# A Conformer/S5 encoder trunk: the second MLP's second product and the final norm with tokens on partitions, three quarters of the product by Strassen's algorithm

## The chip, the cores and the metric

The kernel runs on one core of a Trainium2 chip. The metric is device time in microseconds (us) of one execution. Engines are named as in the profile: PE (TensorE, matmuls), PEld (its weight loads), DVE (VectorE), ACT (ScalarE), POOL (GpSimd), SP (the queue that starts most DMA transfers).

## The reference

One sequence of 512 tokens, 1024 channels, two layers. What matters here is the end of the second layer and the final norm; everything ahead of it (convolution and retention in layer 0, its MLP, the S5 state space layer and its gated unit) is untouched.

```python
h = _rmsnorm(x, norm_g[layer, 1]) * (1.0 + scale_f) + shift_f
x = x + gate_f * (jnp.square(jax.nn.relu(h @ w_fc1[layer])) @ w_fc2[layer])   # 1024 -> 4096 -> 1024
...
return _rmsnorm(x, norm_f)
```

All of it is float32. `gate_f` is one number for each channel.

## The kernel before

The residual stream `self.x` lies as eight tiles of 128 channels (partitions) by 512 tokens. A float32 product is made of three matmuls on halves: each operand is split into a rounded `hi` and a rest `lo` (type float32r), and `mm3` (line 198) adds hi x hi, hi x lo and lo x hi. A weight piece of 128 x 1024 is loaded by the SP queue (`load_unit`), its `hi` is a copy by ACT (line 194), its `lo` a subtraction by DVE (line 189); this is a split unit. `Stream` loads and splits some units ahead of use.

The MLP (`mlp`, line 756) goes through the 4096 hidden channels in four quarters. A quarter has eight units of the first product (24 matmuls each, weights stationary, the 512 tokens moving): relu and square on ACT (lines 801, 806), then split (lines 809, 810). Then eight units of the second product, one for each output tile of 128 channels; results of the first three quarters are partly held in PSUM (`held`), partly added to `self.x` by DVE at once (line 826, with the gate). At its beginning the reciprocal root of the norm (`rstd`) is hidden behind 48 matmuls on un-normed tiles of the first two units (`ahead`), and `norm_tiles` (lines 317 to 338) makes the eight normed tiles while four units run side by side (`group=[4, 1]`, line 817).

After the second MLP `run` (from line 1674) makes the final norm: squares are summed over channels by matmuls with a column of ones (`stats`, `col_sums`), DVE and ACT make the reciprocal root (`rsqrt`, lines 246 to 261), matmuls spread it over the partitions (`bcast`), DVE scales eight tiles (line 1679), and two queues write them out.

The order of instructions on each engine is a compiler's: it follows the program's order as priority, and pulls forward what is ready in its own timing model. Instructions marked `keep_in_program_order` (all SP loads among them) stay in order. Tiles come from pools with a fixed number of buffers (`ps`: eight PSUM banks; `wk`: eight work tiles; `wh` and `wl`: four each; `raw`: seven; `x`: ten).

## Time and profile before

| | |
|---|---|
| time, median of 3 runs | 1204.96 us (1204.0 to 1205.41) |
| profiled execution, its own time | 1205.55 us |
| its span, first to last instruction | 1203.8 us |
| mean granted clock of TensorE | 0.979 |
| busy, share of the span | PE 96%, DVE 72%, ACT 39%, POOL 9% |
| matmuls | 6830 |
| DMA | 223.58 MB, 186 GB/s mean |

The second MLP begins at about 840 us; its last matmul ends at 1188.7 us. A matmul's own duration overlaps with that of the next, so a busy PE says only that PE had no pause; its pace is read from the distance of starts. The granted clock is a share of 2.4 GHz. In a list of groups, `out<-in` are the program's tile names, then partitions x elements, the count, and after the bar busy time and mean duration of one in ns.

### The profile page before, as it was taken

Reading aid. Unit: us, or ns where it says so; the run is one execution under the profiler, and the core shown is the slowest. Engines: PE = TensorE matmul, PEld = TensorE weight load, DVE = VectorE, ACT = ScalarE, POOL = GpSimd, SP = SyncE. Lnnn points to the kernel's source line nnn. Section 1 sums busy time; section 2 is a strip of 40 time slices with the busy share of each in tenths; the row PEclk is TensorE's granted clock in tenths of the full one; section 3 lists DMA queues with packets and bytes.
Section 4 is the critical chain, followed back from the end, with each engine's and each line's share of the span. In section 5 each row is a group of like instructions: output and inputs, shape, how many; then the busy total and the mean of one; then the engine's idle time right before and its main releaser. Section 6 shows DMA issues by size and latency. Waiting matters only on the chain.

```text
span 1203.8 us, 17697 instructions
## 1 busy us (share of the span) xinstructions
PE 1160.8 (96%) x6830; PEld 929.4 (77%) x6830; DVE 864.0 (72%) x1602; ACT 470.5 (39%) x744; POOL 108.9 (9%) x222
## 2 busy tenths in 40 slices
PE   6999999999999999999999899999999999999996
PEld 4777756777888888878777678788888888888885
DVE  6899995999998898798968999498552332332343
ACT  4423322455523423512423756344451532422530
POOL 0000000000002222243422100000000000000000
PEclk7999999999999999999999989999999999999997
DMA  9755341545337689889797968376343333333201
GB/s 352 266 175 192 134 161 47 189 138 200 107 127 245 196 277 276 286 263 312 218 337 240 405 237 346 123 251 213 148 140 105 88 105 89 104 91 103 70 1 70
DMA packets 65668, 223.58 MB, mean 186 GB/s; under 512 B 11136, under 2 KB 11520, under 8 KB 63536
## 3 DMA queue, kind: packets, MB, share of 16 engines
q1 hardware_dynamic: 48528, 174.63, 42.2%
q0 software_dynamic: 16480, 46.79, 12.6%
q8 instruction: 53, 0.87, 0.3%
q10 hardware_dynamic: 576, 1.05, 0.2%
q14 instruction: 31, 0.25, 0.1%
HBM read 197.77 MB, written 29.82 MB: 189 GB/s over the span
## 4 chain that ended last, share of the span: by engine, by line
PE 82%; DVE 8%; DMA 6%; issue 2%; ACT 1%; SPq 0%; POOL 0%; DVEq 0%; POOLq 0%; ACTq 0%
PE ps L167 81%; DVE wk L1291 2%; DMA raw<-adn 1%; DMA d_wi<-eb 1%; DVE w L861 1%; DMA bt<-bt 1%; DVE wl L189 1%; DVE xt L1421 1%; DVE hx L1291 1%; DMA d_t<-d_kk 1%; PE ps L1247 1%; DVE eb L861 1%; DMA raw<-adt 1%; DMA raw<-fc 0%; DMA x<-x 0%
## 5 line engine op out<-in xcount | busy, mean ns | idle before, releaser
L194 ACT CAST wh<-raw 128x1024 fp32r<-128x1024 f32 x169 | 176.8, 1051 | 504.4 <-PE ps L167 439.5
L189 DVE TENSOR_TENSOR wl<-raw,wh 128x1024 fp32r<-128x1024 f32 x169 | 206.0, 1222 | 174.3 <-ACT wh L194 172.1
L167 PE MATMUL ps<-hh,wh 128*128 128x512 f32 x808 | 317.3, 399 | 3.7 <-ACT hh L334 1.7
L167 PE MATMUL ps<-hl,wh 128*128 128x512 f32 x808 | 317.5, 393 | 1.6 <-DVE hl L235 1.2
L167 PE MATMUL ps<-hh,wl 128*128 128x512 f32 x808 | 316.2, 392 | 0.8 <-DVE wl L189 0.8
L167 PE MATMUL ps<-fl,wh 128*128 128x512 f32 x544 | 212.4, 391 | 2.5 <-DVE fl L810 2.5
L167 PE MATMUL ps<-fh,wh 128*128 128x512 f32 x544 | 212.9, 393 | 0.0
L167 PE MATMUL ps<-fh,wl 128*128 128x512 f32 x544 | 212.3, 391 | 0.0
L167 PEld LDWEIGHTS ps<-hh,wh 128*128 128x128 f32 x808 | 152.4, 189 | 41.7 <-issue 3.1
L167 PEld LDWEIGHTS ps<-hl,wh 128*128 128x128 f32 x808 | 152.9, 189 | 34.3 <-DVE hl L235 1.6
L167 PEld LDWEIGHTS ps<-hh,wl 128*128 128x128 f32 x808 | 152.6, 189 | 33.6 <-DVE wl L189 1.6
L167 PEld LDWEIGHTS ps<-fl,wh 128*128 128x128 f32 x544 | 102.5, 188 | 24.4 <-DVE fl L810 3.5
L167 PEld LDWEIGHTS ps<-fh,wh 128*128 128x128 f32 x544 | 102.4, 188 | 22.0 <-issue 1.0
L167 PEld LDWEIGHTS ps<-fh,wl 128*128 128x128 f32 x544 | 102.4, 188 | 21.3
L535 DVE SCALAR_TENSOR_TENSOR cacc<-apad,cvw,cacc 128x512 f32<-128x512 f32 x120 | 83.7, 746 | 0.0
L826 DVE SCALAR_TENSOR_TENSOR x<-ps,mod,x 128x512 f32<-128x512 f32 x40 | 29.9, 748 | 63.1 <-PE ps L167 63.0
L810 DVE TENSOR_TENSOR fl<-wk,fh 128x512 fp32r<-128x512 f32 x64 | 44.1, 689 | 17.3 <-ACT fh L809 17.3
L277 ACT ACTIVATE wk<-x 128x512 f32<-128x512 f32 x35 | 22.1, 630 | 59.0 <-DVE x L826 30.2
L861 DVE TENSOR_TENSOR w<-pb,bt 128x512 f32<-128x512 f32 x64 | 41.4, 687 | 4.7 <-DMA bt<-bt 4.2
L433 DVE SCALAR_TENSOR_TENSOR raw<-raw,x 128x512 f32<-128x512 f32 x52 | 33.2, 687 | 11.9 <-DMA raw<-adt 9.3
L806 ACT ACTIVATE wk<-wk 128x512 f32<-128x512 f32 x64 | 40.7, 636 | 1.5
L809 ACT CAST fh<-wk 128x512 fp32r<-128x512 f32 x64 | 39.8, 622 | 1.7
(240 smaller groups left out, 1265.9 us busy)
## 6 DMA issues: line engine op xcount, KB each, us to landing
raw<-fc SPq DMA_DIRECT2D x128, 512.0 KB, 4.3
raw<-adn SPq DMA_DIRECT2D x50, 512.0 KB, 4.9
raw<-adt SPq DMA_DIRECT2D x34, 512.0 KB, 4.8
pb<-d_pw POOLq DMA_DIRECT2D x32, 256.0 KB, 8.6
bt<-bt POOLq DMA_DIRECT2D x16, 512.0 KB, 9.4
d_e<-eb POOLq DMA_DIRECT2D x16, 512.0 KB, 4.3
d_wi<-eb POOLq DMA_DIRECT2D x16, 512.0 KB, 8.1
wi<-d_wi SPq DMA_DIRECT2D x8, 1024.0 KB, 5.5
```

The lines of the kernel that those rows point to most:

```text
L167: i = self.nc.tensor.matmul(out, lhsT=lhsT, rhs=rhs, start=start, stop=stop, **kw)
L189: self.keep(self.nc.vector.tensor_tensor(lo, raw, hi.bitcast(F32), SUB))
L194: self.keep(self.nc.scalar.copy(hi, raw))
L277: nc.scalar.activation(sq, t, AF.Square)
L433: self.keep(nc.vector.scalar_tensor_tensor(half, half, 1.0, self.cb[k], MUL, MUL, accum_out=v[:, 2 * k + h:2 * k + h + 1]))
L535: nc.vector.scalar_tensor_tensor(ac, ap[:, t:t + S], cvw[:, i * TAPS + t:i * TAPS + t + 1], ac, MUL, ADD)
L806: nc.scalar.activation(f, r, AF.Square)
L809: nc.scalar.copy(hi, f)
L810: nc.vector.tensor_tensor(lo, f, hi.bitcast(F32), SUB)
L826: nc.vector.scalar_tensor_tensor(self.x[m], ps, gate[:, m:m + 1], self.x[m], MUL, ADD)
L861: V.tensor_tensor(o, x, y, op)
L1291: pin(nc.vector.tensor_tensor(*args))
```

## The change

`mlp(1)` and the final norm in `run` are replaced by `mlp_last`; the beginning of the MLP moves unchanged into `mlp_begin`, which both use. In `mlp_last`:

- The residual stream is transposed to tokens on partitions, four tiles `xt` of 128 tokens x 1024 channels, by 32 PE transposes and eight ACT copies.
- The second product has the hidden tile as the stationary operand and rows of `w_fc2` (128 x 1024, loaded as they are) as the moving one.
- Hidden channels 0 to 3071 go in four chunks of three pairs of 128. A pair's product, [512 tokens x 256] times [256 x 1024], is taken as 2 x 2 blocks of [256 x 128] and [128 x 512] by Winograd's form of Strassen's algorithm: `lefts` makes the sums and differences of hidden blocks and splits them, `right` those of weight blocks in place, `split_items` splits two of these at a time, and each of the seven products has two token tiles of three matmuls. Products 1, 6, 7 and 4 run on in the same two PSUM banks, 5 and 3 in two others, 2 in two more; after the last pair of a product `put` reads its banks and adds them to `cs`, eight tiles for the four output blocks. Each chunk has six first-product units ahead of its products, one of them (from the second chunk on) made ahead of product 4 of the chunk before, at `n == 18`.
- The last 1024 hidden channels are a plain product (`plain`) with eight PSUM banks, its weight rows multiplied by the gate ahead of the split. Meanwhile `add_sums` adds gate x `cs` to `xt`.
- The last three of its eight units are done for one token tile after the other, and each token tile is then normed (sums along the free dimension, by ACT) and written out.
- The gate reaches the free dimension through DRAM (`d_g`) on POOL's queue. The weight order is a list of loads and a list of splits (`Jobs`). The memory set aside for POOL's DMA descriptors is cut to 4096 bytes a partition.

```diff
+class Jobs:
...
+    def ahead(self, loads, splits):
+        while self.splits and len(self.ready) < splits:
+            f, n = self.splits.pop(0)
+            self.load(n)
+            self.ready.append(f())
+        if self.splits:
+            self.load(self.splits[0][1] + loads)
+    def __next__(self):
+        self.ahead(1, 1)
+        return self.ready.pop(0)
...
+    def mlp_last(self, out):
...
+        CH, NP, PL = 4, 3, 24
...
+        def row(u):
+            def f():
+                rows[u] = wr.tile([P, 1024], F32, name="wr", tag="wr")
+                self.load(rows[u], a["fc2_1"][u])
+            return f
...
+        def split_plain(u):
+            def f():
+                r = rows.pop(u)
+                for h in range(2):
+                    g = slice(h * 512, h * 512 + 512)
+                    V.tensor_tensor(r[:, g], r[:, g], gt[h], MUL)
+                return self.split_unit(r)
+            return f
...
+        def right(p, i):
+            r11, r12, r21, r22 = (reg(i, s, h) for s in range(2) for h in range(2))
+            if p == 1:
+                return r11
+            if p == 2:
+                return r21
+            if p == 3:
+                return r22
+            o, x, y = {5: (r11, r12, r11), 6: (r11, r22, r11), 7: (r12, r22, r12), 4: (r21, r21, r11)}[p]
+            V.tensor_tensor(o, x, y, SUB)
+            return o
+        slot = {1: 0, 2: 1, 4: 2, 5: 3, 6: 4, 7: 5, 3: 6}
+        items = [(1, 0), (1, 1), (5, 0), (5, 1), (1, 2), (5, 2)] + [(p, i) for p in (2, 6, 3, 7, 4) for i in range(NP)]
+        def split_items(q, its):
+            def f():
+                hi = self.wh.tile([P, 1024], F32R, name="wh", tag="wh")
+                lo = self.wl.tile([P, 1024], F32R, name="wl", tag="wl")
+                for n, (p, i) in enumerate(its):
+                    r, h = right(p, NP * q + i), slice(n * 512, n * 512 + 512)
+                    A.copy(hi[:, h], r)
+                    V.tensor_tensor(lo[:, h], r, hi[:, h].bitcast(F32), SUB)
+                return hi, lo
+            return f
...
+        loads, splits = [], []
+        at = {}
+        for q in range(CH):
+            u = 2 * NP * q
+            for n in (0, 1, 2, 3, "r0", "r1", 4, "r2", 5, "r3", "r4", "r5"):
+                m = u + (n if isinstance(n, int) else int(n[1]))
+                loads.append(fc1(m) if isinstance(n, int) else row(m))
+                at[isinstance(n, int), m] = len(loads)
+        for m in range(PL, 32):
+            loads.append(fc1(m))
+            at[True, m] = len(loads)
+        for m in range(PL, 32):
+            loads.append(row_plain(m))
+            at[False, m] = len(loads)
+        for q in range(CH):
+            u = 2 * NP * q
+            splits += [(split_fc1(m), at[True, m]) for m in range(u + (q > 0), u + 2 * NP)]
+            for n in range(0, len(items), 2):
+                if n == 18:
+                    splits.append((split_fc1(u + 2 * NP), at[True, u + 2 * NP]))
+                its = items[n:n + 2]
+                splits.append((split_items(q, its), max(at[False, u + 2 * i + s] for _, i in its for s in range(2))))
+        splits += [(split_fc1(m), at[True, m]) for m in range(PL + 1, 32)]
+        splits += [(split_plain(m), at[False, m]) for m in range(PL, 32)]
+        src = Jobs(loads, splits)
+        src.ahead(1, 1)
+        rb, hs, cm, pss = self.mlp_begin(1, src, shift)
...
+        self.stack.pop_all().close()
+        st = ExitStack()
+        keep = st.enter_context(tc.tile_pool(name="keep", bufs=1, reuse_waits="tile"))
+        xt = [keep.tile([P, D], F32, name=f"xt{t}") for t in range(4)]
+        st2 = ExitStack()
+        wr = st2.enter_context(tc.tile_pool(name="wr", bufs=2 * NP, reuse_waits="tile"))
+        st2.enter_context(tc.tile_pool(name="fpad", bufs=1, side="right", reuse_waits="tile")).tile([P, 8], F32, name="fpad")
+        ap = st2.enter_context(tc.tile_pool(name="ap", bufs=1, side="right", reuse_waits="tile"))
+        for t in range(4):
+            for h in range(2):
+                ps = self.psum()
+                for n in range(4):
+                    nc.tensor.transpose(ps[:, n * P:(n + 1) * P], self.x[4 * h + n][:, t * P:(t + 1) * P], self.ident)
+                A.copy(xt[t][:, h * 512:(h + 1) * 512], ps)
+        nc.gpsimd.dma_start(self.d_g.rearrange("m p -> p m"), gate)
+        gt = [self.xp.tile([P, S], F32, name="x", tag="x") for _ in range(2)]
+        for h in range(2):
+            nc.gpsimd.dma_start(gt[h], self.d_g[4 * h:4 * h + 4].rearrange("(o m) p -> o (m p)", o=1).broadcast_to([P, S]))
...
+        def hidden(u, ps):
+            r = self.work()
+            if u >= 2:
+                A.activation(r, ps, AF.Relu)
+            else:
+                V.tensor_tensor(r, ps, rb, MUL)
+                A.activation(r, r, AF.Relu, bias=cm[:, u:u + 1])
+            f = self.work()
+            A.activation(f, r, AF.Square)
+            return f
+        def unit(u):
+            w = next(src)
+            ps = self.psum()
+            for k in range(8):
+                self.mm3(ps, w, k, hs[k], k == 0, k == 7)
+            return hidden(u, ps)
+        def lefts(i, fa, fb):
+            s12, s34 = self.work(), self.work()
+            a0, a1 = slice(0, 256), slice(256, 512)
+            tt = V.tensor_tensor
+            tt(s12[:, a0], fa[:, a1], fb[:, a1], ADD)
+            tt(s12[:, a1], s12[:, a0], fa[:, a0], SUB)
+            tt(s34[:, a0], fa[:, a0], fa[:, a1], SUB)
+            tt(s34[:, a1], fb[:, a0], s12[:, a1], SUB)
+            hi = ap.tile([P, 7 * 256], F32R, name=f"ah{i}")
+            lo = ap.tile([P, 7 * 256], F32R, name=f"al{i}")
+            for n, (o, s) in enumerate(((slice(0, 256), fa[:, a0]), (slice(256, 768), fb), (slice(768, 1280), s12),
+                                        (slice(1280, 1792), s34))):
+                A.copy(hi[:, o], s)
+                tt(lo[:, o], s, hi[:, o].bitcast(F32), SUB)
+            return hi, lo
...
+        cs = {}
+        chain = {}
+        def put(b, p, q, neg=False):
+            for t in range(2):
+                ps = chain[p][t]
+                if (b, t) not in cs:
+                    cs[b, t] = self.xp.tile([P, S], F32, name="x", tag="x")
+                    A.copy(cs[b, t], ps)
+                else:
+                    V.tensor_tensor(cs[b, t], ps, cs[b, t], ADD)
+        def ends(p, q):
+            for b in {1: [(0, 0)], 2: [(0, 0)], 5: [(1, 1)], 6: [(0, 1)], 7: [(1, 1)], 3: [(0, 1)], 4: [(1, 0)]}[p]:
+                put(b, {1: 0, 6: 0, 7: 0, 4: 0, 5: 1, 3: 1, 2: 2}[p], q)
+        fa = None
+        fr = {}
+        for u in range(2):
+            fr[u] = hidden(u, pss[u])
+        for q in range(CH):
+            lf = []
+            for i in range(NP):
+                for u in (2 * (NP * q + i), 2 * (NP * q + i) + 1):
+                    if u not in fr:
+                        src.ahead(3, 3)
+                        fr[u] = unit(u)
+                lf.append(lefts(i, fr.pop(2 * (NP * q + i)), fr.pop(2 * (NP * q + i) + 1)))
...
+            for n, (p, i) in enumerate(items):
+                c = {1: 0, 6: 0, 7: 0, 4: 0, 5: 1, 3: 1, 2: 2}[p]
+                if n == 18:
+                    u = 2 * NP * (q + 1)
+                    fr[u] = unit(u)
+                if n % 2 == 0:
+                    src.ahead(3, 3)
+                    w = next(src)
+                if i == 0 and p in (1, 5, 2):
+                    chain[c] = [self.psum(), self.psum()]
+                h = slice(n % 2 * 512, n % 2 * 512 + 512)
+                first, last = i == 0 and p in (1, 5, 2), i == NP - 1
+                for t in range(2):
+                    o = slot[p] * 256 + t * P
+                    ah, al = (x[:, o:o + P] for x in lf[i])
+                    kw = {} if p in (1, 5, 2) else dict(skip_group_check=True)
+                    self.mm(chain[c][t], ah, w[0][:, h], first, False, **kw)
+                    self.mm(chain[c][t], ah, w[1][:, h], False, False, **kw)
+                    self.mm(chain[c][t], al, w[0][:, h], False, last, **kw)
+                if last:
+                    ends(p, q)
+        st2.close()
+        with tc.tile_pool(name="fpad", bufs=1, side="right", reuse_waits="tile") as fpad, \
+                tc.tile_pool(name="fq", bufs=8, side="right", reuse_waits="tile") as fq, \
+                tc.tile_pool(name="fin", bufs=1, reuse_waits="tile") as fin:
+            fpad.tile([P, 8], F32, name="fpad")
+            nf = fin.tile([P, D], F32, name="nf")
+            nc.gpsimd.dma_start(nf, a["nf"].broadcast_to([P, D]))
...
+            def add_sums():
+                t, h = adds.pop(0)
+                m, g = self.work(), slice(h * 512, h * 512 + 512)
+                V.tensor_tensor(m, cs[(t // 2, h), t % 2], gt[h], MUL)
+                V.tensor_tensor(xt[t][:, g], xt[t][:, g], m, ADD)
+            fs = []
+            for u in range(PL, 32):
+                src.ahead(3, 3)
+                f = fr.pop(u) if u in fr else unit(u)
+                hi = fq.tile([P, 512], F32R, name="fh", tag="fh")
+                lo = fq.tile([P, 512], F32R, name="fl", tag="fl")
+                A.copy(hi, f)
+                V.tensor_tensor(lo, f, hi.bitcast(F32), SUB)
+                fs.append((hi, lo))
+                add_sums()
+            src.ahead(3, 3)
+            ps = {(t, h): self.psum() for t in range(4) for h in range(2)}
+            def plain(n, t, h, w):
+                ah, al = (x[:, t * P:(t + 1) * P] for x in fs[n])
+                wh, wl = (x[:, h * 512:h * 512 + 512] for x in w[:2])
+                self.mm(ps[t, h], ah, wh, n == 0, False)
+                self.mm(ps[t, h], ah, wl, False, False)
+                self.mm(ps[t, h], al, wh, False, n == 7)
+            E = 5
+            for n in range(E):
+                src.ahead(3, 3)
+                w = next(src)
+                for t in range(4):
+                    for h in range(2):
+                        plain(n, t, h, w)
+            src.ahead(3, 3)
+            ws = [next(src) for _ in range(8 - E)]
+            A.activation(self.work()[:, 0:1], self.one, AF.Sqrt)
+            for t in range(4):
+                s = self.sm.tile([P, 2], F32, name="ss", tag="ss", bufs=4)
+                for h in range(2):
+                    for n, w in enumerate(ws):
+                        plain(E + n, t, h, w)
+                    x = xt[t][:, h * 512:h * 512 + 512]
+                    V.tensor_tensor(x, ps[t, h], x, ADD)
+                    A.activation(self.work(), x, AF.Square, accum_out=s[:, h:h + 1])
+                r = self.rsqrt(s, 1, 1.0 / D, True)
+                for h in range(2):
+                    g = slice(h * 512, h * 512 + 512)
+                    o = self.work()
+                    V.scalar_tensor_tensor(o, xt[t][:, g], r, nf[:, g], MUL, MUL)
+                    (nc.sync if h else nc.scalar).dma_start(out[t, :, g], o)
+        st.close()
...
+            self.d_g = dr.tile([NT, P], F32, name="d_g")
...
-            self.nf = self.m8[:, 0:NT]
-            nc.sync.dma_start(self.nf, a["nf"])
-            self.mlp(1)
-            self.stack.pop_all().close()
-            pb = self.rstd()
-            for i in range(8):
-                o = self.work()
-                nc.vector.scalar_tensor_tensor(o, self.x[i], self.nf[:, i:i + 1], pb, MUL, MUL)
-                (nc.sync if i % 2 else nc.scalar).dma_start(out[i], o)
+            self.mlp_last(out)
...
-    nc = bacc.Bacc("TRN2", target_bir_lowering=False, num_devices=1)
+    nc = bacc.Bacc("TRN2", target_bir_lowering=False, num_devices=1, dynamic_dma_scratch_size=4096)
...
-    o = build(lambda tc, a, out: Kern(tc, a).run(out), arrays, (NT, P, S))
-    o = o.reshape(D, L, NK).transpose(2, 1, 0).reshape(1, S, D)
+    o = build(lambda tc, a, out: Kern(tc, a).run(out), arrays, (4, P, D))
+    o = o.reshape(L, NK, D).transpose(1, 0, 2).reshape(1, S, D)
```

## Rows read from the trace of the kernel before

**Rows 1.** The page: span, busy time of each engine, clock in tenths by slice.
```profile
span 1203.8 us, 17697 instructions
...
PE 1160.8 (96%) x6830; PEld 929.4 (77%) x6830; DVE 864.0 (72%) x1602; ACT 470.5 (39%) x744; POOL 108.9 (9%) x222
...
PEclk7999999999999999999999989999999999999997
```
**Rows 2.** Busy us by stretch; columns: stretch, length, engines, clock, DMA share, GB/s.
```profile
300.00:400.00 100.00, 100.00 (x470) 81.38 (x470) 90.82 (x222) 40.10 (x59) 10.80 (x20) 1.00 0.51 165
...
900.00:1000.00 100.00, 100.00 (x443) 82.84 (x442) 32.92 (x33) 34.01 (x43) 0.00 (x0) 1.00 0.31 95
```
**Rows 3.** The chain that ended last, in order of time: start, us, what.
```profile
779.81 408.88 PE ps L167 x1872
...
1188.72 0.76 DVE x L826
...
1189.50 0.64 ACT wk L277
...
1191.27 0.17 DVE rv L252
...
1192.93 2.09 PE ps L167 x8
...
1196.45 3.95 DVE wk L1679 x6
```
**Rows 4.** Groups of instructions from 850 us on, kept apart by shape.
```profile
L167 PE MATMUL ps<-fl,wh 128*128 128x512 f32 x256 | 99.4, 389 | 0.0
...
L189 DVE TENSOR_TENSOR wl<-raw,wh 128x1024 fp32r<-128x1024 f32 x59 | 72.2, 1225 | 137.6 <-ACT wh L194 135.9
L194 ACT CAST wh<-raw 128x1024 fp32r<-128x1024 f32 x59 | 62.1, 1055 | 189.8 <-PE ps L167 188.5 <-DMA raw<-fc 1.4
...
L810 DVE TENSOR_TENSOR fl<-wk,fh 128x512 fp32r<-128x512 f32 x32 | 22.1, 692 | 17.0 <-ACT fh L809 17.0
```
**Rows 5.** Instructions in order of time: start, us, what; 38 starts apart.
```profile
1179.67 0.39 PE L167 MATMUL ps<-fh,wh 128*128 128x512 f32 x1
...
1188.29 0.39 PE L167 MATMUL ps<-fh,wl 128*128 128x512 f32 x1
```
**Rows 6.** PE in order of time around transposes of the S5 layer.
```profile
660.43 1.03 PE L1334 MATMUL ps<-ident,x 128*128 128x128 f32 x8
661.31 0.95 PE L167 MATMUL ps<-cc,ssq 128*128 128x1 f32 x8
...
734.40 0.66 PE L1334 MATMUL ps<-ident,x 128*128 128x128 f32 x4
734.99 1.21 PE L167 MATMUL ps<-hl,wi 128*64 128x64 f32 x34
```
**Rows 7.** Busy us by stretch: after 660 us, and while norm tiles are made.
```profile
660.00:665.00 5.00, 5.00 (x59) 3.93 (x57) 1.93 (x11) 2.89 (x6) 0.26 (x1) 1.00 1.00 406
665.00:670.00 5.00, 3.04 (x58) 2.59 (x56) 4.81 (x11) 3.47 (x10) 0.88 (x2) 0.89 1.04 432
670.00:675.00 5.00, 5.00 (x68) 3.43 (x64) 4.60 (x8) 1.93 (x7) 2.81 (x6) 0.77 1.01 409
...
850.00:855.00 5.00, 5.00 (x28) 4.30 (x28) 4.50 (x8) 2.77 (x6) 0.00 (x0) 1.00 1.01 401
```
**Rows 8.** DVE in order of time, instructions without a wait between them.
```profile
831.96 2.35 DVE L189 TENSOR_TENSOR wl<-raw,wh 128x1024 fp32r<-128x1024 f32 x2
834.23 0.69 DVE L281 TENSOR_TENSOR ssq<-ssq,wk 128x512 f32<-128x512 f32 x1
834.84 0.75 DVE L753 SCALAR_TENSOR_TENSOR fl<-x,gs,fh 128x512 fp32r<-128x512 f32 x1
```
**Rows 9.** Groups by shape over the whole span: a DVE instruction of 256 columns.
```profile
L1291 DVE TENSOR_TENSOR hl<-hl,wk 128x256 f32<-128x256 f32 x2 | 0.8, 425 | 0.1
```
**Rows 10.** POOL in order of time: its last transfers.
```profile
672.19 4.47 POOL L1117 DMA_DIRECT2D d_t<-d_kk x8 [6.31 <-DMA d_kk<-d_kr]
```
**Rows 11.** DMA issues: count, KB each, us to landing.
```profile
d_t<-d_kk POOLq DMA_DIRECT2D x32, 128.0 KB, 6.9
```

82 lines of the change are left out of this document (54 added, 28 removed).

## The prediction

> **What bounds the kernel now.** I read the page first: TensorE (PE) is busy 1160.8 of 1203.8 us and the clock is near full almost everywhere [rows 1]. Then the windows: from 900 to 1000 us, inside the second MLP, PE is 100.00 of 100 us busy at granted clock 1.00, while VectorE (DVE) has 33 us and ScalarE (ACT) 34 us of work and the DMA moves 95 GB/s [rows 2]. Then the chain of waits in order of time: its last long piece is 408.88 us of PE, without a break until 1188.7 us, and after it comes a tail that PE hardly shares [rows 3]. So in this stage every matmul taken off PE is time gained, as long as DVE, which gets most of the new work, does not become the later one; and the tail from 1188.69 us to the end, 15.1 us, is a serial sum of its own.
>
> A matmul's row says 389 ns [rows 4], but they overlap. The price is the distance of their starts: 1179.67 to 1188.29 us over 38 steps, 0.2268 us each [rows 5].
>
> **Part 1, fewer matmuls.** The first product stays at 32 units of 24 matmuls, 768. The second had 8 outputs x 4 quarters x 24 = 768, three groups of 256 [rows 4]. Now three quarters of it, 12 pairs of units, take 7 block products x 2 token tiles x 3 = 42 matmuls for a pair instead of 48, so 504; the plain quarter takes 8 x 8 x 3 = 192. That is 696: 72 matmuls fewer, of the same shape (128x128 against 512 columns). 72 x 0.2268 = **16.3 us saved**. The Trainium skill's page "TensorE: Matmul & The Clock Gate", section "Back-to-back issue gap", gives some 131 ns for a matmul of 512 columns in a sustained stream of weight load and matmul; by it the saving would be 9.4 us (an estimate from that page) and the time some 7 us later. The trace disagrees with that figure, with 0.2268 us.
>
> **Part 2, the transposes.** To put tokens on partitions, 32 transposes of 128x128 are added on PE behind `mlp_begin`. The trace has the same form (`ident,x`): eight start at 660.43 and the next instruction at 661.31, 0.110 us each; four take 734.40 to 734.99, 0.147 us each [rows 6]. So 3.5 to 4.7 us; I take 4.0. PE has no hole there for them to fall into: 850 to 855 us, while the norm tiles are made, shows PE 5.00 of 5 busy [rows 7]. It is so because four units run side by side there; the new code writes one `unit` after the other, which alone would wait for a norm tile every 1.3 us (two DVE instructions at 0.66, the spacing in the last row of [rows 3]). The transposes, and units 3 and 4 if they are pulled forward as in the trace, fill that. If nothing hides and nothing is lost the price is 4.0; 0 if they fall wholly into such a hole. Their eight evacuations by ACT, 8 x 0.64 at the price of a 512-wide ACT instruction [rows 3], are 5 us in a stretch in which ACT is a little over half busy, 2.77 of 5 us [rows 7].
>
> **Part 3, the tail.** Before, after the last matmul (1188.69): x update 0.76, square 0.64, column sums, from 1191.27 the reciprocal root until 1192.93, broadcast 2.09, then eight scalings until 1196.45 + 3.95 = 1200.40, and 3.40 until the last output has landed [rows 3]. After, the norm is along the free dimension, so column sums and broadcast go, and three of the four token tiles are finished under the matmuls of the next (18 matmuls = 4.1 us each). The last one: add 0.76, square 0.64, root chain 1192.93 - 1191.27 = 1.66, two scalings of 0.66 with 0.1 for the first's start, landing 3.4, some 0.1 for hand-overs: 8.0. **15.1 - 8.0 = 7.1 us saved.** Bounds: 6 if the tile before still holds DVE, 8 if half the landing (two outputs instead of eight) goes.
>
> **Part 4, DVE work, which decides.** For a chunk of three pairs: six splits of 1024 columns; `lefts` has 3 x (5 of 256 + 3 of 512); `right` 12 of 512; `split_items` 21 of 512; `put` 14 of 512 (in the first chunk eight of these are ACT copies). Sum: 56 x 0.692 + 15 x 0.425 + 6 x 1.225 = 52.5 us by durations [rows 4, 9]. But independent DVE instructions start closer than they last: the 0.69 us one at 834.23 is followed at 834.84, two of 1024 take 2.35 [rows 8]. With 0.08 off each of the 77: 46.3 us. PE's share of a chunk is (144 + 126) x 0.2268 = 61.2 us, so DVE is 76 to 86% full: it fits as a mean, and 300 to 400 us shows DVE at 90.82 with PE at 100.00 [rows 2]. ACT has six splits at 1.055 and about 12 + 9 + 21 of 512 [rows 3, 4], some 35 us of 61, and is not the bound.
>
> Inside a chunk it is tighter. From the end of the sixth first-product unit, the three ready pairs included, the 17 items ahead of the last of product 7 give PE 17 x 6 x 0.2268 = 23.1 us. In that time DVE has to do the third `lefts`, 14 splits, 7 `right` and up to 10 `put`: 34 of 512 and 5 of 256, 25.6 us by durations and 22.5 by starts. So a chunk loses between 0 and 2.5 us; then the extra unit at n = 18, 24 matmuls or 5.4 us, lets DVE catch up. Which one holds depends on how many of these instructions wait for each other (`right`, then ACT's copy, then the subtraction). I take 1 us a chunk, nearer to the starts row since the order lets independent ones go between: **4 us lost, bounds 0 and 10**.
>
> **Edits at nothing.** Weight loads: the same bytes in pieces of 512 KB, at 95 GB/s in this stage [rows 2]; the SP queue now also waits for `wr` slots, and behind such a wait stands the next chunk's fifth first-product unit, needed a full phase later. Its cover is some 20 us; without it a piece's landing would show. The gate goes to DRAM and back on POOL's queue, whose last work so far ends at 677 us [rows 10], some 200 us ahead of the first use. `add_sums` and the gate's multiplications (1.4 us a unit) lie in the last quarter, where DVE has 3 us of work for 5.4 of PE. The smaller descriptor area acts on POOL's transfers in the S5 preparation; the trace doesn't show that resource. Lower bound 0 (an area cannot be faster for being small). Upper: eight transfers that POOL issues in 4.47 us [rows 10], if each waited for the one before, 6.9 us to landing [rows 11], would take 8 x 6.9 = 55, 51 us more. I take 0: these rows show issues back to back, and nothing in them waits for room.
>
> **Sum**, against the profiled execution, 1205.55 us: 1205.55 - 16.3 - 7.1 + 4.0 + 4.0 = 1190.15. The median of the runs is 0.6 below that execution: 1189.6, said as **1190 us**.
>
> **The rivals.**
> (a) DVE sets the pace of every product phase: the 25.6 us end. Loss 10 instead of 4, plus 2 of waiting at the start for norm tiles: 1190 + 8 = 1198. For it: the margin is thinner than the spread of the two prices. Against it: DVE at 91% and PE at 100% side by side [rows 2].
> (b) Slower: the running sum of products 1, 6, 7 and 4 stays in the same two banks, so PE cannot start 6, 7 or 4 before DVE's `put` has read them. If three prepared pairs, up to 4 x 0.69 each, stand ahead of it in DVE's queue, it ends 8.3 + 1.4 = 9.7 us late; covered are 5.4 us (product 1 to 6), 4.1 (6 to 7) and 5.4 (7 to 4). A chunk loses up to 4.3 + 5.6 + 4.3 = 14 us. It decides from 4.85 us a chunk, where it eats the 19.4 us of parts 1 to 3. At half its price, 7 a chunk: 1205.55 - 19.4 + 28 - 0.6 = 1213. Against it: the written order puts each `put` ahead of the splits that are called later, so mostly one pair stands ahead.
> (c) The clock. From 660 to 665 us, with transposes and one-column matmuls, it stays 1.00; in the two windows after, with small matmuls, it is 0.89 and 0.77, that is partly at 1.2 instead of 2.4 GHz [rows 7]. If 32 transposes in a row do the same, by those rows 0.11 x 5 + 0.23 x 5 = 1.7 us are lost, and up to 3.4 if it comes twice: 1192 to 1193. The Trainium skill's "TensorE: Matmul & The Clock Gate", section "Part 4: PE-mode transpose", says that transposes don't count as activity for the clock in the way that matmuls do; that would bring this case. First-product matmuls stand between them, which speaks against.
> (d) The small descriptor area stalls POOL: up to 51 us, 1241; at a quarter of it 1203.
> (e) The change doesn't do what it says: the new matmuls, whose weights are slices of wider tiles, start at longer distance. 696 of them by 0.01 us more is 7 us, 1197.
>
> **How the numbers follow.** Forecast 0.58 (1185 to 1194), (a) 0.19, (b) 0.09, (c) 0.07, (d) 0.03, (e) 0.04. Low end: no DVE loss, part of the transposes hidden, 1205.55 - 23.4 + 2.5 - 0.6 = 1184. High end: (a) with the upper bounds of transposes and clock, 1200; beyond lie (b), most of (d) and a little of (a), with what lies below 1184 some 0.17. A measurement can tell about 0.2%, 2.4 us, from no change. Faster: forecast, (a), (c), (e), less a little, 0.86; within 0.2%: 0.03; slower: (b) and most of (d), 0.11.
>
> **What would show it.** In the changed trace: 504 + 192 matmuls of the second product at 0.227 us; 32 transposes between 846 and 866 us in 4 us; the third MLP phase with PE near 100% and DVE at 75 to 85%; PE's waits for `wl` or for `cs` under 2.5 us a chunk; last matmul to end 8 us. Wrong it would be if PE's idle time behind DVE comes to over 10 us, if the stages ahead of 840 us move, or if the start-to-start distance grows.

## The result, and the profile after

| | before | after |
|---|---|---|
| median, side by side | 1205.18 us (4 runs) | 1187.43 us (4 runs, 1186.73 to 1190.22) |
| ratio | | 0.9845, interval 0.983 to 0.9859 |
| measured again | 1204.85 us (11 runs) | 1187.87 us (6 runs), 0.9856, 0.9831 to 0.988 |
| profiled execution, span | 1203.8 us | 1188.4 us (time 1190.22) |
| mean granted clock | 0.979 | 0.985 |
| second MLP, first broadcast matmul to last matmul | 342.71 us | 330.69 us |
| tail, last matmul to the end | 15.12 us | 8.66 us |
| begin of the second MLP | 845.97 us | 849.05 us |

The forecast was 1190 us, range 1184 to 1200, faster. The last three rows are the ones to work with. The stage got 12.0 us shorter and the tail 6.5, together 18.5; the span fell by only 15.4, because in this one execution of after the second MLP began 3.1 us later. The code ahead of it is unchanged, and in the twelve executions shown further down this begin lies anywhere between 843.24 and 848.64 us; the same program, profiled a second time, has it at 846.76. So these 3.1 us are spread between executions and no effect of the change. From here on, kernels are compared by stage and tail, which repeat to 0.1 us (that second profile of after: 330.73 and 8.71), and not by single times, which scatter by up to 7 us. The span is read to 0.1 us, so a difference of 0.1 us between two tails says nothing.

The page of after, lines that answer to [rows 1]:

```profile
span 1188.4 us, 17980 instructions
...
PE 1149.7 (97%) x6766; PEld 918.0 (77%) x6766; DVE 980.1 (82%) x1865; ACT 513.6 (43%) x855; POOL 111.4 (9%) x226
...
PEclk9999999899999999999999999999999999999999
```

DVE has 116 us more and is still not what PE waits for. The chain that ended last (start, us, what), to set beside [rows 3]:

```profile
760.25 89.87 PE ps L193 x448
856.48 1.97 PE ps L983 x16
858.45 321.31 PE ps L193 x1416
1180.76 1.41 DVE wk L1135 x2
```

Where there was one piece of PE to 1188.7 us there are two with the transposes (L983) between them, and the last piece, 1416 matmuls in 321.31 us, runs at 0.2269 us each, the distance of [rows 5]: from there to the end PE loses next to nothing. The stage by stretch (stretch, length, busy us of PE, PEld, DVE, ACT, POOL with instructions, granted clock, DMA share, GB/s), beside [rows 7] for its begin; the last row is a whole chunk:

```profile
849.05:855.05 6.00, 6.00 (x94) 4.91 (x92) 4.10 (x7) 4.08 (x9) 0.00 (x0) 1.00 0.55 176
855.05:858.20 3.15, 2.81 (x25) 2.58 (x25) 3.15 (x7) 3.15 (x7) 0.91 (x1) 1.00 1.02 410
...
941.58:1002.78 61.20, 61.20 (x271) 50.69 (x270) 47.22 (x77) 31.59 (x52) 0.00 (x0) 1.00 0.28 103
```

A chunk takes 61.20 us from its first product to the next chunk's, which is 270 x 0.2268 = 61.2: no loss at all, with 77 DVE instructions of 47.22 us (predicted: 77, 46.3 to 52.5). Only the first chunk takes 61.5, 0.3 more. In the whole stage the list of PE's waits has a single row (engine, what it waited with, for whom: us, times, longest):

```profile
PE ps L983 <- ACT xt L984: 0.3, 1, 0.3
```

That is the second half of the transposes waiting for an evacuation of PSUM. The groups of the stage, by shape (count | busy us, mean ns | idle before):

```profile
L193 PE MATMUL ps<-wl,ah 128*128 128x512 f32 x168 | 64.7, 389 | 0.0
...
L936 DVE TENSOR_TENSOR wl<-wr,wh 128x512 fp32r<-128x512 f32 x84 | 55.6, 687 | 12.5 <-ACT wh L935 12.3
L1038 DVE TENSOR_TENSOR x<-ps,x 128x512 f32<-128x512 f32 x48 | 32.6, 687 | 6.1 <-PE ps L193 6.1
```

With a third group of 168 (`wh,ah`) and `wh,al` not shown, 3 x 168 = 504 product matmuls at the old 389 ns, 84 split halves, 48 additions of `put`, as counted.

### The profile page after: what moved, and what is told of

It is laid out like the page before. It is cut to its first block, busy times and chain, and to the rows that moved or that the text cites. A ratio compares the mean times of both kernels' runs of the same rounds, so it can differ in the third digit from the quotient of the medians.

```text
span 1188.4 us, 17980 instructions
## 1 busy us (share of the span) xinstructions
PE 1149.7 (97%) x6766; PEld 918.0 (77%) x6766; DVE 980.1 (82%) x1865; ACT 513.6 (43%) x855; POOL 111.4 (9%) x226
## 3 DMA queue, kind: packets, MB, share of 16 engines
q10 hardware_dynamic: 576, 1.05, 0.2%
## 4 chain that ended last, share of the span: by engine, by line
PE 81%; DVE 9%; DMA 5%; issue 2%; ACT 2%; SPq 0%; DVEq 0%; ACTq 0%
PE ps L193 80%; DMA raw<-fc 2%; DVE wk L1586 2%; DMA raw<-adt 1%; DVE wl L215 1%; DVE w L1156 1%; DMA d_wi<-eb 1%; DVE xt L1716 1%; DMA hh<-adn 1%; DVE hx L1586 1%; PE ps L1542 1%; DVE eb L1156 0%; ACT wh L220 0%; DMA x<-x 0%; DVE ssq L307 0%
## 5 line engine op out<-in xcount | busy, mean ns | idle before, releaser
L193 PE MATMUL ps<-fl,wh 128*128 128x512 f32 x288 | 113.7, 395 | 3.5 <-DVE fl L812 3.5
L193 PE MATMUL ps<-fh,wh 128*128 128x512 f32 x288 | 114.2, 399 | 0.0
L193 PE MATMUL ps<-fh,wl 128*128 128x512 f32 x288 | 113.5, 394 | 0.0
L935 ACT CAST wh<-wr 128x512 fp32r<-128x512 f32 x84 | 48.5, 620 | 58.6 <-PE ps L193 58.4
L193 PEld LDWEIGHTS ps<-fl,wh 128*128 128x128 f32 x288 | 54.7, 190 | 15.4 <-DVE fl L812 4.5
L936 DVE TENSOR_TENSOR wl<-wr,wh 128x512 fp32r<-128x512 f32 x84 | 55.6, 687 | 12.5 <-ACT wh L935 12.3
L193 PE MATMUL ps<-wl,ah 128*128 128x512 f32 x168 | 64.7, 389 | 0.0
L193 PEld LDWEIGHTS ps<-fh,wh 128*128 128x128 f32 x288 | 54.7, 190 | 12.2 <-issue 1.0
L193 PE MATMUL ps<-wh,ah 128*128 128x512 f32 x168 | 63.9, 390 | 0.0
L193 PE MATMUL ps<-wh,al 128*128 128x512 f32 x168 | 63.4, 389 | 0.0
L459 DVE SCALAR_TENSOR_TENSOR raw<-raw,x 128x512 f32<-128x512 f32 x52 | 33.2, 689 | 12.4 <-DMA raw<-adt 9.8
```

The costliest lines, as they stand in the source:

```text
L193: i = self.nc.tensor.matmul(out, lhsT=lhsT, rhs=rhs, start=start, stop=stop, **kw)
L459: self.keep(nc.vector.scalar_tensor_tensor(half, half, 1.0, self.cb[k], MUL, MUL, accum_out=v[:, 2 * k + h:2 * k + h + 1]))
L935: A.copy(hi[:, h], r)
L936: V.tensor_tensor(lo[:, h], r, hi[:, h].bitcast(F32), SUB)
```

## The experiments

**Seven products undone** (`eight`). Everything else of the change stays, the tokens on partitions, the transposes, the tail; the block products are the plain eight. `lefts` then only splits, `put` and `chain` keep four token tiles for each half of the columns, and the extra unit stands at `n == 8`.

```diff
-        items = [(1, 0), (1, 1), (5, 0), (5, 1), (1, 2), (5, 2)] + [(p, i) for p in (2, 6, 3, 7, 4) for i in range(NP)]
+        items = [(h, 2 * i + s) for h in range(2) for i in range(NP) for s in range(2)]
...
-                    r, h = right(p, NP * q + i), slice(n * 512, n * 512 + 512)
+                    r, h = rows[2 * NP * q + i][:, p * 512:(p + 1) * 512], slice(n * 512, n * 512 + 512)
...
-                for t in range(2):
-                    o = slot[p] * 256 + t * P
+                for t in range(4):
+                    o = i % 2 * 512 + t * P
```

> The change with eight block products instead of seven for the same three quarters: no sums or differences of blocks, 72 matmuls more. Theory (each matmul taken off PE is 0.2268 us gained, DVE pays nothing of it back): the MLP's matmul stage is 16.3 us longer than in the changed kernel, 347 us instead of 330.7 from the broadcast of the norm to the last matmul; time some 1203.7 us. Rival (the gain is the new layout and the tail, and the seven products' block sums on DVE eat most of the 16.3): under 10 us longer, below 1197 us.

Measured: 1202.97 us (10 runs), 0.9985 of before, interval 0.9971 to 0.9999. The stage is 346.70 us, 16.0 longer than after; each chunk takes 65.28 us, 288 x 0.2267. The theory holds. So the seven products are worth 16.0 us, and all the rest of the change only 2.4 (stage +4.0 against before, tail -6.4).

**The tail without its cover** (`tail_late`). All eight units of the plain quarter go over the eight banks before any token tile is finished.

```diff
-            E = 5
+            E = 8
```

> The change with all eight plain units done for all token tiles before any is normed (E = 8 instead of 5): same matmuls, the four norms then stand one after the other. Theory (three of four token tiles are finished under matmuls): the time from the last matmul to the end is 8.66 us plus three times about 3.9 us of DVE (two adds, root chain, two scalings), 20 us; 11 to 12 us slower. Rival (the outputs' landing sets the tail, which is the same either way): under 3 us slower.

Measured: 1192.07 us (2 runs); stage 330.72, tail 14.64. The tail grows by 6.0 us, half of what was expected and more than the rival's 3. DVE's scalings in that tail (start, us, what; two more follow at the same distance):

```profile
1174.98 1.41 DVE L1135 SCALAR_TENSOR_TENSOR wk<-xt,rr,nf 128x512 f32<-128x512 f32 x2
...
1177.96 1.41 DVE L1135 SCALAR_TENSOR_TENSOR wk<-xt,rr,nf 128x512 f32<-128x512 f32 x2
```

A token tile costs 2.98 us here, not more: the additions and squares of the first tiles still run under the last matmuls, and only root chain and scalings stand one behind the other. So three tiles under the matmuls of the next are worth 6.0 us. That is nearly the whole gain of the tail: with tokens on partitions alone it would be 15.12 - 14.64 = 0.5.

**Without the transposes** (`no_turn`). `xt` is filled from `self.x` by the eight ACT copies as they are, which leaves the transposition out of the computation.

```diff
-                ps = self.psum()
-                for n in range(4):
-                    nc.tensor.transpose(ps[:, n * P:(n + 1) * P], self.x[4 * h + n][:, t * P:(t + 1) * P], self.ident)
-                A.copy(xt[t][:, h * 512:(h + 1) * 512], ps)
+                A.copy(xt[t][:, h * 512:(h + 1) * 512], self.x[4 * h + t])
```

> The change without the 32 transposes: the eight ACT copies read the residual tiles themselves, so what is added in the end is the untransposed residual (that part of the computation is left out). Theory (PE has no hole there, 4.0 us predicted): the stage from the broadcast of the norm to the last matmul is 4 to 4.3 us shorter than 330.7. Rival (the transposes fill a wait for the norm tiles, since the units come one after the other): 0 to 1.5 us shorter, and PE shows waits for hh or hl instead.

Measured: 1186.18 us (2 runs), stage 328.70, 2.0 shorter, which is neither expectation. By places: the first product starts 27.00 us after the stage's begin instead of 31.03, so 4.0 us are gained there; but the first chunk then takes 63.54 us instead of 61.5. There PE waits, released by ACT each time (start, us, what, idle before it and for whom):

```profile
889.79 0.50 PE L193 MATMUL ps<-wh,ah 128*128 128x512 f32 x1 [0.37 <-ACT ah L1020]
...
891.36 0.73 PE L193 MATMUL ps<-wh,ah 128*128 128x512 f32 x2 [0.36 <-ACT wh L935]
...
893.25 0.50 PE L193 MATMUL ps<-wh,ah 128*128 128x512 f32 x1 [0.44 <-ACT x L1033]
```

So the transposes do cost PE their full 4 us, and without them half of it comes back as a loss in the first chunk. That ACT is too slow for that chunk is not shown: it stood idle for 2.78 us up to 888.08 us, until PE freed a `wh` buffer, while DVE had no pause at all (columns as in the windows above):

```profile
885.00:890.00 5.00, 4.63 (x21) 3.52 (x20) 5.00 (x10) 2.22 (x5) 0.00 (x0) 1.00 0.01 2
```

**The descriptor area alone** (`ring`): the kernel before, with POOL's area cut.

```diff
-    nc = bacc.Bacc("TRN2", target_bir_lowering=False, num_devices=1)
+    nc = bacc.Bacc("TRN2", target_bir_lowering=False, num_devices=1, dynamic_dma_scratch_size=4096)
```

> The kernel before with nothing changed but the memory for POOL's DMA descriptors, 4096 bytes a partition. Theory: no change, within 0.2% of before, and the second MLP begins at the same time within the spread of runs. Rival: POOL's transfers wait for room, the S5 preparation gets longer, and the 3 us by which the second MLP began later in the profiled run of the changed kernel come from there: 2 to 50 us slower.

Measured: 1205.84 us (10 runs), ratio 0.9999, interval 0.9983 to 1.0016; stage 342.73, tail 15.09. The cut costs nothing in nine of these runs, 1203.64 to 1207.88 us, from which the ratio is made. The tenth took 4050.44 us, and why is not shown. None of the 40 runs of the kernels with the change, which all have the cut, did that.

**Why no chunk loses anything** (`pin_right`). In the trace of after, the subtractions of `right` stand well ahead of the place at which the program writes them. Here they are held in program order.

```diff
-            V.tensor_tensor(o, x, y, SUB)
+            self.tc.keep_in_program_order(V.tensor_tensor(o, x, y, SUB))
```

> The change with the differences of weight blocks (right) held in the written order on DVE, so that they can't be pulled ahead of the products. In the changed kernel nine of a chunk's twelve run before its first product. Theory A (PE lost nothing in the chunks because the compiler spread this work into the first-product phase): the burst is then as I sized it, 0 to 2.5 us lost in a chunk, stage from the broadcast of the norm to the last matmul 332 to 341 us, 334 likely, against 330.7, and PE waits for wl or wh. Rival B (DVE has room in the products in any order, at 0.61 us an instruction): stage within 0.5 us of 330.7.

Measured: 1199.86 us (one run); stage 342.09, 11.4 longer, just above theory A's range; chunks of 61.66, 64.92 and 64.96 us. `right` on DVE in chunk 2, whose first product starts at 941.58 us, in after:

```profile
927.10 1.89 DVE L924 TENSOR_TENSOR wr<-wr 128x512 f32<-128x512 f32 x3
...
929.24 0.69 DVE L924 TENSOR_TENSOR wr<-wr 128x512 f32<-128x512 f32 x1
...
932.54 1.29 DVE L924 TENSOR_TENSOR wr<-wr 128x512 f32<-128x512 f32 x2
...
937.98 1.41 DVE L924 TENSOR_TENSOR wr<-wr 128x512 f32<-128x512 f32 x2
...
940.37 0.69 DVE L924 TENSOR_TENSOR wr<-wr 128x512 f32<-128x512 f32 x1
...
943.42 1.29 DVE L924 TENSOR_TENSOR wr<-wr 128x512 f32<-128x512 f32 x2
...
947.43 0.69 DVE L924 TENSOR_TENSOR wr<-wr 128x512 f32<-128x512 f32 x1
```

and with `right` held, where the first product of the chunk starts at 940.00 us (the first three of the twelve, and the last):

```profile
925.52 0.68 DVE L924 TENSOR_TENSOR wr<-wr 128x512 f32<-128x512 f32 x1
...
930.36 0.68 DVE L924 TENSOR_TENSOR wr<-wr 128x512 f32<-128x512 f32 x1
...
935.91 0.69 DVE L924 TENSOR_TENSOR wr<-wr 128x512 f32<-128x512 f32 x1
...
973.93 0.68 DVE L924 TENSOR_TENSOR wr<-wr 128x512 f32<-128x512 f32 x1
```

Nine of twelve run ahead of the products in after, and the last 6 us into them; held, three do, and the last comes 34 us in. The same DVE instructions (47.23 us in such a chunk against 47.22) then cost 3.7 us a chunk. DVE isn't fuller for it: in the first 23.1 us of the products of chunk 2 it is busy for 20.79 us in after (first row), where PE loses nothing, and for 17.75 us with `right` held, where PE does:

```profile
941.58:964.68 23.10, 23.10 (x103) 19.15 (x102) 20.79 (x36) 11.72 (x20) 0.00 (x0) 1.00 0.24 85
940.00:963.10 23.10, 22.67 (x97) 17.45 (x95) 17.75 (x31) 8.90 (x16) 0.00 (x0) 1.00 0.00 1
```

What is late is a chain: ACT's copy waits for `right`, the subtraction for the copy, PE for both. From the list of waits in the stage, ACT's wait for `right` (after has no such row) and PE's own:

```profile
ACT wh L935 <- DVE wr L924: 59.3, 33, 6.9
...
PE ps L193 <- DVE x L1038: 2.5, 7, 0.4
PE ps L193 <- ACT wh L935: 0.7, 3, 0.2
PE ps L193 <- ACT wh L220: 0.7, 3, 0.2
```

PE's waits are spread over seven late `put` additions and late splits; they add up to a third of the loss, the rest shows only as wider distances of starts. The seven stand where a product takes over the banks of another, at the first matmul behind a chunk's 90th or 108th: 0.42 us at 961.71 and 0.33 at 973.47 in chunk 2. So with the same amount of work, what decides is where `right` stands on DVE.

**How much room a chunk has** (`double1`, `double2`). The subtraction that makes `lo` is written twice for one of each two items (11 more a chunk), or for both (21 more).

```diff
                     V.tensor_tensor(lo[:, h], r, hi[:, h].bitcast(F32), SUB)
+                    if n == 0:
+                        V.tensor_tensor(lo[:, h], r, hi[:, h].bitcast(F32), SUB)
```

> The change with the first subtraction of each pair of weight blocks done twice on DVE (same values, 11 more of 512 columns in a chunk, 6.7 us). Mean DVE load of a chunk 46.3 + 6.7 = 53.0 of 61.2 us. Theory A (the mean decides, since work is spread over the chunk): 0 to 1 us lost in a chunk, stage under 335. Rival B (the burst of the products decides, 22.5 + 5.2 = 27.7 us of DVE in 23.1): 2 to 4.6 us a chunk, stage 338 to 349.

> The same with every subtraction of weight blocks done twice (21 more in a chunk, 12.8 us): mean DVE load 59.1 of 61.2 us. Theory A (the mean decides): it just fits in the mean, but four buffers can't hold a chunk's work, so 1 to 4 us a chunk are lost, stage 335 to 347. Rival B (the burst decides: 22.5 + 10.4 = 32.9 us in 23.1): 7 to 10 us a chunk, stage 358 to 370.

Measured, one run each: 1191.34 us with 11 more, stage 335.23, chunks of 65.73, 61.3 and 61.3 us; 1212.16 us with 21 more, stage 357.71, chunks of 71.94, 68.14 and 65.86. With 11 more, theory A holds from the second chunk on, and the first loses what B gave; with 21 more the stage is just under B's range and far over A's. PE's waits with 21 more, by what it waited for:

```profile
PE ps L193 <- DVE wl L937: 5.2, 8, 1.3
PE ps L193 <- DVE x L1039: 3.1, 1, 3.1
...
```

From the second chunk on, 11 more DVE instructions of 0.61 to 0.69 us (7 us) cost 0.1 us, and 21 more (13 to 14 us) cost 4.7 to 6.9. So from the second chunk on a chunk of after has room for some 7 us more of DVE work, where the prediction saw a margin of +0.6 to -2.5 in its burst. The first chunk has none: it loses 4.2 us with 11 more. It is the chunk in which PE waits in `no_turn` too, again with no pause on DVE (5.00 of 5 us from 880 to 890 us with 11 more). Why it loses only 0.2 us with `right` held is not shown.

Not all of this loss is waiting. With 11 more, PE waits 1.05 us up to 894.89 us, and behind that wait its clock is granted almost wholly at the lower of its two levels, 1.2 instead of 2.4 GHz:

```profile
894.90:898.40 3.50, 3.50 (x8) 2.79 (x9) 3.50 (x7) 0.00 (x0) 0.00 (x0) 0.51 0.37 129
```

Eight matmuls take 3.5 us there instead of 8 x 0.2268 = 1.8, so some 1.7 of the 4.2 us, an estimate from these rows, are the clock's. With 21 more the first two chunks have such stretches too (0.52 from 966.5 to 972.5 us, behind a wait of 3.1 us), and the third has none, in spite of a wait of 1.2 us: its loss of 4.7 us holds no such share.

**The extra unit ahead of product 4** (`no_cover`). The unit at `n == 18` goes back to the next chunk, so that nothing written covers the hand-over of the banks from product 7 to 4.

```diff
-                if n == 18:
-                    u = 2 * NP * (q + 1)
-                    fr[u] = unit(u)
```

> The change with the extra first-product unit not written between products 7 and 4 of a chunk but in the next chunk's first-product phase: product 4 then follows product 7 in the same banks. Theory A (the hand-over of the banks costs what DVE needs to read them): PE waits for two reads of 0.69 us and what stands ahead of them, 1.5 to 3 us a chunk, stage 337 to 343 and waits of PE behind DVE's addition to cs. Rival B (the compiler pulls first-product matmuls of the next chunk into that gap by itself): stage within 1 us of 330.7.

Measured: 1187.48 us (one run), stage 330.74, chunks of 61.55, 61.2 and 61.2 us. No effect: rival B holds, the compiler pulls the unit forward by itself. In after its 24 matmuls stand among the products of chunk 2, two at 961.98 us and the others from 966.51 on, ahead of the last 18 product matmuls (product 4). Without the written order, 18 matmuls of it stand there from 965.36 on (the chunk's first product is at 938.84), and not ahead of product 4: nine of the last 18 product matmuls start at 963.32, without a pause behind the 108th, and nine at 969.44. By the times of `put`, these are its two token tiles: DVE has read the first one's bank by 962.17 us, while the matmuls of product 7's second token tile ran, and reads the second one's from 964.39 on. The hand-over of the banks costs nothing in either form. It does cost in `pin_right`, where `put` is late.

**A shorter tail** (`e4`, `e4_act`, `e4_last`). In after, the last token tile's root chain does not follow its squares at once. DVE and ACT at the end (start, us, what):

```profile
1179.78 0.69 DVE L1129 TENSOR_TENSOR xt<-ps,xt 128x512 f32<-128x512 f32 x1 [0.32 <-PE ps L193]
...
1180.76 1.41 DVE L1135 SCALAR_TENSOR_TENSOR wk<-xt,rr,nf 128x512 f32<-128x512 f32 x2
1182.09 0.15 DVE L278 TENSOR_SCALAR rv<-ss 128x1 f32<-128x1 f32 x1
...
1183.75 1.41 DVE L1135 SCALAR_TENSOR_TENSOR wk<-xt,rr,nf 128x512 f32<-128x512 f32 x2
...
1181.04 0.19 ACT L1130 ACTIVATION_READ_ACCUMULATOR wk<-xt 128x1 f32 x1
```

The sum of squares is there at 1181.23 us (ACT, the row out of order at the end), but DVE scales the token tile before until 1182.1.

```diff
-            E = 5
+            E = 4
```

> Edit: E = 4, so that four units of the plain quarter instead of three are done for one token tile after the other: 24 matmuls, 5.44 us, stand between the ends of two token tiles instead of 18, 4.08 us. Theory: in the changed kernel the last token tile's root chain starts 0.86 us after its sum of squares is there (1181.23 to 1182.09 us), because DVE makes the two scalings of the token tile before; with 1.36 us more between the tiles these are done earlier, and the tail from the last matmul to the end falls from 8.66 to 7.8 us, the stage stays at 330.7 us. Rival: the order on DVE is the compiler's and not a matter of time, the scalings of the tile before stay ahead of the last root chain: tail 8.6 to 8.7 us. A second rival: four units made ahead instead of three take all four split buffers, PE waits for a split, the stage gets 1 us longer or more.

Measured: 1188.29 us (one run), stage 330.67, tail 7.60. The last two scalings start 2.95 us after the last matmul instead of 4.01. The theory holds; the gain, 1.06, is a little above the 0.86 expected, as the chain's step for the first half (L278) no longer stands behind the scalings either.

```diff
+                    if h:
+                        V.tensor_tensor(x, x, nf[:, 512:1024], MUL)
...
+                    if h:
+                        A.activation(o, xt[t][:, g], AF.Identity, scale=r)
+                    else:
+                        V.scalar_tensor_tensor(o, xt[t][:, g], r, nf[:, g], MUL, MUL)
```

> Edit: E = 4, and of the two scalings of a token tile the second is made on ACT: DVE multiplies that half by the norm's weight while ACT still squares and sums, then ACT multiplies by the root, beside DVE's scaling of the first half. Theory: the two scalings, one behind the other 1.41 us, become 0.75 us beside each other, the tail is 7.8 - 0.66 = 7.1 us, so 1.5 us less than the changed kernel's 8.66, and the stage stays at 330.7 us; the median 1186 against 1187.4 us. Rival: the additional multiplication on DVE comes between the square and the root chain of the same tile and costs 0.3 to 0.7 us: tail 7.4 to 7.8 us.

Measured: 1188.06 us (5 runs), 0.9849 of before, interval 0.983 to 0.9869; tail 9.66, worse than both expectations. ACT's scaling of the tile before (start 1178.13, 0.72 us) now stands ahead of the last tile's squares, whose second one starts 2.13 us after the last matmul, against 0.80 in `e4`. The last run takes that away: only the last token tile's second half goes to ACT, from a tile of its own, and each engine's half has its own queue.

```diff
+                if t == 3:
+                    xn = self.work()
+                    V.tensor_tensor(xn, x, nf[:, 512:1024], MUL)
...
+                    if t == 3 and h:
+                        A.activation(o, xn, AF.Identity, scale=r)
```

> Edit: E = 4 as in e4, and for the last token tile alone the second scaling is made on ACT, from a copy of that half that DVE has multiplied by the norm's weight into a tile of its own; ACT starts the transfer of its own half, SP that of the first. Theory: the run with ACT scalings for every token tile lost because ACT's scaling of the tile before stood ahead of the last tile's squares, because the multiplication in place waited for the square, and because ACT's start of the first half's transfer stood behind its scaling; none of the three is left here, so the last two scalings lie beside each other: tail 7.60 - 0.66 = 6.9 us, stage 330.7 us. Rival: the compiler puts the additional multiplication ahead of the root chain's last steps where it delays them, or the last transfer takes as long as in that run (4.0 us after the scaling instead of 3.2): tail 7.5 to 8.0 us.

Measured: 1188.21 us (6 runs, 1183.75 to 1190.7), 0.985 of before, interval 0.9827 to 0.9873; stage 330.67, tail 7.68. Both scalings end 3.73 us after the last matmul, where the second one ends at 4.36 in `e4`, as meant, and the tail did not move: it is in the rival's range. The last 4 us, by half microseconds (columns as above; the last is GB/s), in `e4`, where the scalings end at 1182.60 and at 1183.26:

```profile
1183.00:1183.50 0.50, 0.00 (x0) 0.00 (x0) 0.26 (x1) 0.00 (x0) 0.00 (x0) 0.50 0.08 29
1183.50:1184.00 0.50, 0.00 (x0) 0.00 (x0) 0.00 (x0) 0.00 (x0) 0.00 (x0) 0.50 0.99 365
1184.00:1184.50 0.50, 0.00 (x0) 0.00 (x0) 0.00 (x0) 0.00 (x0) 0.00 (x0) 0.50 1.01 381
1184.50:1185.00 0.50, 0.00 (x0) 0.00 (x0) 0.00 (x0) 0.00 (x0) 0.00 (x0) 0.50 0.73 275
```

and in `e4_last`, where both end at 1180.85:

```profile
1181.30:1181.80 0.50, 0.00 (x0) 0.00 (x0) 0.00 (x0) 0.00 (x0) 0.00 (x0) 0.50 0.22 82
1181.80:1182.30 0.50, 0.00 (x0) 0.00 (x0) 0.00 (x0) 0.00 (x0) 0.00 (x0) 0.50 1.02 389
1182.30:1182.80 0.50, 0.00 (x0) 0.00 (x0) 0.00 (x0) 0.00 (x0) 0.00 (x0) 0.50 1.01 381
1182.80:1183.30 0.50, 0.00 (x0) 0.00 (x0) 0.00 (x0) 0.00 (x0) 0.00 (x0) 0.50 0.55 197
```

In both the data begin to move some 0.9 us after the first scaling has ended, the two halves take 1.5 us from first to last packet, with all DMA engines full in between (share 0.99 to 1.02, 365 to 389 GB/s), and the end comes 1.5 to 1.6 us later. In `e4` the first half moves from 1183.47 to 1184.31 us and the second from 1184.16 on, so the second scaling, done at 1183.26, was hidden behind the start of the first half's transfer all along. The first scaling ends at the same distance from the last matmul in both runs, 3.70 us.

The changed kernel itself, beside `e4_last`:

> The changed kernel as it is, for a comparison on one chip. Expected: stage 330.7 us, tail 8.66 us, both the same to 0.1 us, while the start of the second MLP lies anywhere between 843 and 849 us. With e4_last 1.7 us shorter in its tail, its median should be 1.7 us lower; with single times spread over some 5 us, five runs of each may not show it.

Measured: 1187.87 us (6 runs), stage 330.73, tail 8.71. So `e4` and `e4_last` have the shortest tails, 1.0 to 1.1 us below after by the trace; times of five or six runs do not show a difference of that size, and no version is claimed to beat after by them.

## Why the prediction was right

The forecast of 1190 us lies 2.6 us above the median, within its range, and its direction holds. By its steps:

**Part 1, fewer matmuls: right.** 16.3 us predicted; 16.0 by undoing it, which is 16.3 less the 0.3 that the first chunk loses in after and not in `eight`. The distance of starts, 0.2268 us, was the price to take, not the 389 ns of a row. By the rule of the Trainium skill, page "TensorE: Matmul & The Clock Gate", section "Back-to-back issue gap", it would have been 9.4, an estimate from that page; these runs disagree, with 0.2268 us for each of 270 matmuls in a chunk.

**Part 2, the transposes: the sum right.** 4.0 us predicted, bounds 0 and 4.7. Read from after (start, us, what):

```profile
853.24 0.74 PE L983 MATMUL ps<-ident,x 128*128 128x128 f32 x5
853.82 0.51 PE L193 MATMUL ps<-cc,adr 128*128 128x1 f32 x4
854.19 0.53 PE L983 MATMUL ps<-ident,x 128*128 128x128 f32 x3
854.55 0.50 PE L193 MATMUL ps<-cc,adr 128*128 128x1 f32 x4
855.05 1.09 PE L983 MATMUL ps<-ident,x 128*128 128x128 f32 x8
856.48 1.97 PE L983 MATMUL ps<-ident,x 128*128 128x128 f32 x16 [0.34 <-ACT xt L984]
858.20 0.48 PE L193 MATMUL ps<-hh,wh 128*128 128x512 f32 x1
```

From 853.24 to 858.20 us, less 0.87 for the two groups of other matmuls between, is 4.09 us. What the prediction also said, that they fill a hole in which PE would wait for norm tiles, was wrong in its place: without them PE is busy at once with normed units, and the loss of 2.0 us comes 37 us later, in the first chunk. The stage's balance closes: -16.3 + 4.1 + 0.3 (the first chunk) = -11.9, measured -12.0.

**Part 3, the tail: right mechanism, mis-sized.** 15.1 - 8.0 = 7.1 predicted, 15.12 - 8.66 = 6.5 measured, inside the bounds of 6 and 8. The term "hand-overs, some 0.1" is the one that was too small: the wait for DVE alone is 0.86. Its lower bound named the reason, DVE still held by the tile before; `e4` measures it at 1.06. And one term was not on the path: of the two scalings only the first counts, the second lies beside the start of the first half's transfer (`e4_last`).

**Part 4, DVE in the products: wrong, 4 us predicted and 0.3 measured, all of it in the first chunk.** The step that failed is the count of the burst, "14 splits, 7 `right` and up to 10 `put`" in 23.1 us, and the 1 us a chunk taken from it. Totals and durations held (77 instructions, 47.2 us), and so did the splits and `put`: 14 and 11 in that stretch of chunk 2. But there are three `right` in it, not seven. The count left them near the place where the program writes them, while what holds one is its loaded rows and whatever still reads the block that it overwrites: the compiler moved nine of twelve ahead of the products, into the first-product phase, where DVE has room. DVE is busy for 20.79 of the 23.1 us and PE waits for nothing. The chain that the prediction said would decide, `right`, then ACT's copy, then the subtraction, is real: with `right` held it costs 3.7 us a chunk, more than the 2.5 put as the upper end. The prediction knew the rule, that ready instructions are pulled forward, and used it for the units but not for `right`. That the time came out near the forecast all the same is due to the size of this term, 4 us beside 23.4 saved, and owes nothing to this step. (ACT's "some 35 us" of a chunk is 33.2 by its own terms, 6 x 1.055 + 42 x 0.64, and 31.59 in after; nothing hangs on it.)

**Edits at nothing: held.** PE waits for no weight, no gate, no `add_sums` (the one row of waits), and the descriptor area costs nothing (`ring`, nine runs of ten).

**The rivals.** (a) DVE sets the pace: fell in after. Its 1198 is near the 1199.86 us of `pin_right`, but by chance: DVE has pauses there, and the order of its work sets the pace, not the amount. (b) The bank hand-over: fell in after, also without the written cover; it shows in `pin_right`, with waits of 0.42 and 0.33 us a chunk, far from 7. (c) The clock: 1.00 in every stretch from 849.05 us to the last matmul, so it stays at the 2.4 GHz level through the transposes. The Trainium skill's page "TensorE: Matmul & The Clock Gate", section "Part 4: PE-mode transpose", says that the full clock is not engaged for transposes; by that rule some 1.7 to 3.4 us would have been lost, as the prediction worked out. The trace disagrees: 24 of the 32 stand in a row, with one wait of 0.34 us, and the granted clock of that stretch is 1.00 (the second row of windows). The rows name them MATMUL, as all others, so they don't show whether the page's transpose mode is on, and no run shows a longer row. Where the clock did fall in this stage, in `double1` and `double2`, it was behind waits of PE, which the prediction did not price. (d) The descriptor area: fell by nine runs of `ring`; its one long run stays open. (e) Longer distances: fell, 389 ns and 0.2268 us as before.

The error of 2.6 us is thus 3.7 us of DVE loss that did not come, less 0.6 in the tail and 0.1 in part 2, which makes 3.0; the rest is inside the scatter of the times.

## What to carry to other kernels

When an engine is 76 to 86% full in a phase, ask first which of its instructions may run earlier: one that waits only for loaded data and an early split can go into the phase before. Here it counted more whether the compiler may move 12 such instructions (3.7 us a chunk) than whether there are 11 more (0.1 us from the second chunk on); 21 more did cost 4.7 us and over. Test an added piece by taking it away and then look by places, not at the sum: the transposes cost 4.0 us where they stand, and their absence was worth 2.0, because the chunk behind them then waited. At the end of this kernel the transfer of the last outputs is the last stage, and its start hangs on the first of them: making the second one earlier too gave nothing.

## What the runs showed of the hardware

- A transpose of 128x128 in a row of them starts 0.11 to 0.14 us after the one before, about half the 0.2268 us of a matmul with 512 columns, at granted clock 1.00 (after).
- DVE 47 us and ACT 32 us busy beside a PE without a pause for 61.2 us, with 103 GB/s of DMA: none of them slowed the matmuls measurably (0.2267 to 0.2269 us from start to start in after and `eight`).
- Two outputs of 256 KB on two queues, ready 0.7 us apart (`e4`) or together (`e4_last`), take 1.5 us for both, at 365 to 389 GB/s in the full windows, and 1.5 to 1.6 us more until the program's end.
- Behind a wait of 1.05 us in a stretch of matmuls, the granted clock was 0.51 for 3.5 us (`double1`), and behind one of 3.1 us 0.52 for 6 us (`double2`); behind one of 1.2 us in `double2` and those of 0.2 to 0.45 us in `pin_right` and `no_turn` it stayed 1.00.
